# Gates of a recurrent mixer by features, convolution parameters on another queue, and a relative bias stored once

## The chip, the cores and the metric

The kernel runs on one core of a Trainium2 chip, in one launch. The metric is the device time of one execution in microseconds (us). Engines are named as the profile names them: PE is TensorE (PEld its weight loads), DVE is VectorE, ACT is ScalarE, POOL is GpSimd, and SP is SyncE, which here only issues DMAs.

## The reference, cut to what matters

Two layers over 1024 tokens of 1024 features in float32. The first layer mixes tokens by HGRN2, a gated linear recurrence with 8 heads of 128; the second by attention in a window of 128 with 16 query heads and a relative bias. Each layer ends with a gated ConvFFN (a causal convolution of width 3 in it). The parts that the change touches:

```
q, f, i, g = split(h @ w_in)                       # per head 128 columns of each
o = hgrn2_chunkwise(silu(q), 1 - fg, i, log(fg))   # i are the values V
o = o * rsqrt(mean(o**2) + eps)                    # per token and head
o = o * g_norm_w * silu(g)                         # silu(g) is the gate G
mix = o @ w_out
...
logits = q k^T * scale + bias[head, t - s]         # bias: a table of 32 buckets x 16 heads
...
u = conv(h @ w_in, conv_w) + conv_b
```

## The kernel before, in words

All activations live in SBUF (128 partitions, P = 128). Each float32 matmul of a projection is made of three products (`mm3`, lines 171 to 175: high by high, high by low, low by high) of operands that were split into a rounded high part (a cast on ACT, L154 for weights, L199 for activations) and the rest (a subtraction on DVE, L147). `T` is the input by features, high and low; `HL` is a ring of six split weight units; `raw` is a ring of three buffers for weights as they come from DRAM, loaded by SP (L142).

**The HGRN stage** takes about the first 525 us and handles the heads one after the other. For a head there are projections and a recursion. `qf` projects q and f *by features*: the weights stand in PE and 512 tokens of `T` move (`proj_T`, 24 matmuls for half of the tokens). `ig_block` projects the values V and the gate G of one head together, *by tokens*: a block of 128 tokens of `T` stands, and 256 columns of weights move, 128 of V and 128 of G (`proj_tok`, 48 matmuls for two token blocks, four such calls for a head). ACT copies V out of PSUM and makes the sigmoid of G (L694, L695), DVE multiplies it by the projection (L696). `recur`, a generator, is the recursion of a head: column sums and scores on PE (L178), levels of decay products on DVE and POOL (L854, L856, L859), masked placing (L834), states (L930, L932), and at the end the output og of eight token blocks in PSUM, squared and summed by ACT (L945), with POOL making the norm's factor ss (L946, L947), DVE multiplying by G (L948) and by ss (L949), PE transposing og (L182), and ACT scaling it by g_norm_w into Y (L956). For the last head the transposed og goes straight into the high and low parts of T (`split_scaled`, L203 on ACT and L204 on DVE). The parts of Y are then split into T (`Y_to_T`, L199 and L147) for the output projection, whose first products for other heads are made while the last head's recursion still runs.

**What sets the order.** PE's and SP's instructions run in the order in which the program writes them (`manual_schedule`); those of ACT, DVE and POOL are placed by a scheduler within their waits, except in the first block of the program, where ACT and DVE are in written order too. The recursion of head h-1 is woven between the projections of head h by the class `Order`: `od.t` is a clock that adds an estimated cost for each matmul, and after each `mm3` group `od.tick()` lets every waiting generator whose due time is reached write its next piece. A generator's `yield 8.0` is the delay to its next piece. `slot_begin` and `slot_end` put loads, stores (bsd) and sums of FFN weights between the blocks.

`conv_params` is such a generator. When the clock has come to 360, it loads the convolution's weights and biases of both layers in pieces `cr` (88 x 128, two buffers) by ACT's DMA queue, transposes each on PE (L783) and copies it (L784); then it loads rel_bias and a one-hot table, multiplies them on PE (L794) to the bias of each head by distance, and stores that to DRAM as `rbd`, 128 copies of 256 numbers for each of 16 heads (2 MB, L797). In the attention stage (about 1290 to 1455 us) SP loads for each pair of query heads a tile `bf` (L1154) whose partition p is a row shifted by p, and POOL adds it to the scores X (L1212, 32 times), before DVE takes the row maximum (L1216).

Lines of the kernel that the text names are those of the listing here.

## Time and profile before

| | |
|---|---|
| three runs | 2191.42, 2185.72, 2184.57 us |
| median | 2185.72 us |
| profiled execution | 2187.37 us, its span 2185.6 us |
| instructions | 33447 |
| PE rows in program order (matmuls, runs of equal ones merged) | 9831 |
| HGRN stage | 0 to about 525 us |

A profile page gives for each engine the time in which it had work and that time's share of the span. A line of waits reads: engine, the tile it was to write, its line, and behind the arrow what released it (engine or DMA, tile, line), then total us, number and longest. A timeline row is: start, duration, engine, line, operation, output and inputs, shape, count of equal ones in a row, and in brackets the idle time ahead of it with what ended it. A q behind an engine's name (ACTq, SPq) marks DMAs that it issues.

### The profile page before, as it was taken

Reading aid. Unit: us, or ns where it says so; the run is one execution under the profiler, and the core shown is the slowest. Engines: PE = TensorE matmul, PEld = TensorE weight load, DVE = VectorE, ACT = ScalarE, POOL = GpSimd, SP = SyncE. Lnnn points to the kernel's source line nnn. Section 1 sums busy time; section 2 is a strip of 40 time slices with the busy share of each in tenths; the row PEclk is TensorE's granted clock in tenths of the full one; section 3 lists DMA queues with packets and bytes.
Section 4 is the critical chain, followed back from the end, with each engine's and each line's share of the span. In section 5 each row is a group of like instructions: output and inputs, shape, how many; then the busy total and the mean of one; then the engine's idle time right before and its main releaser. Section 6 shows DMA issues by size and latency. Waiting matters only on the chain.

```text
span 2185.6 us, 33447 instructions
## 1 busy us (share of the span) xinstructions
PE 2149.7 (98%) x13263; PEld 1803.4 (83%) x13263; DVE 1739.9 (80%) x2291; ACT 924.5 (42%) x1573; POOL 183.2 (8%) x207
## 2 busy tenths in 40 slices
PE   8999999999999999999999999999999999999998
PEld 7888888988788888887888887778888888888887
DVE  2777666575789988988997766767899888889987
ACT  4333323342744334444343436755654444343431
POOL 0112121110100000000000022211000000000001
PEclk9999999999999999999999999999999999999999
DMA  5554443152223222227845331123123222249663
GB/s 199 192 196 174 155 174 117 59 111 95 96 69 105 87 87 87 87 81 256 298 156 168 106 100 35 35 81 122 68 97 106 78 77 78 87 154 324 202 216 130
DMA packets 231943, 281.10 MB, mean 129 GB/s; under 512 B 29977, under 2 KB 160746, under 8 KB 228970
## 3 DMA queue, kind: packets, MB, share of 16 engines
q1 hardware_dynamic: 228736, 276.53, 38.3%
q10 hardware_dynamic: 3050, 2.43, 0.9%
q8 instruction: 104, 1.70, 0.3%
q14 instruction: 53, 0.43, 0.1%
HBM read 213.90 MB, written 65.01 MB: 128 GB/s over the span
## 4 chain that ended last, share of the span: by engine, by line
PE 82%; DVE 9%; ACT 3%; DMA 3%; issue 2%; POOL 1%; SPq 0%; ACTq 0%; DVEq 0%; POOLq 0%
PE psmm L172 17%; PE psmm L173 17%; PE psmm L174 16%; PE psax L172 8%; PE psax L173 8%; PE psax L174 8%; PE psax L178 3%; PE psmm L178 1%; PE psax L1197 1%; DVE T L147 1%; PE psax L182 1%; DVE Y L477 1%; DVE HL L147 1%; DMA rx<-in_ffn_w_in_dram 1%; ACT Y L247 1%
## 5 line engine op out<-in xcount | busy, mean ns | idle before, releaser
L172 PE MATMUL psmm<-T,HL 128*128 128x512 f32 x768 | 307.5, 400 | 0.0
L173 PE MATMUL psmm<-T,HL 128*128 128x512 f32 x768 | 299.6, 390 | 4.0 <-DVE T L147 2.8
L174 PE MATMUL psmm<-T,HL 128*128 128x512 f32 x768 | 299.8, 390 | 0.0
L477 DVE SCALAR_TENSOR_TENSOR Y<-Y,cwt 128x1023 f32<-128x1023 f32 (+1 forms) x176 | 225.0, 1279 | 40.0 <-ACT Y L475 39.7
L475 ACT ACTIVATE Y<-Y,cwt 128x1024 f32<-128x1024 f32 x88 | 108.9, 1237 | 257.8 <-DVE Y L464 254.3
L172 PE MATMUL psmm<-HL,T 128*128 128x256 f32 (+1 forms) x656 | 199.8, 305 | 1.9 <-ACT T L199 1.7
L174 PE MATMUL psmm<-HL,T 128*128 128x256 f32 (+1 forms) x656 | 195.2, 297 | 1.4 <-DVE T L147 1.4
L173 PE MATMUL psmm<-HL,T 128*128 128x256 f32 (+1 forms) x656 | 195.1, 297 | 1.2 <-DVE HL L147 1.2
L199 ACT CAST HL<-rx 128x1024 fp32r<-128x1024 f32 (+1 forms) x137 | 140.2, 1046 | 124.5 <-DMA rx<-in_ffn_w_in_dram 33.6
L147 DVE TENSOR_TENSOR HL<-rx,HL 128x1024 fp32r<-128x1024 f32 (+1 forms) x137 | 165.7, 1212 | 14.5 <-ACT HL L199 14.0
L174 PEld LDWEIGHTS psmm<-T,HL 128*128 128x128 f32 x768 | 144.2, 188 | 32.4 <-issue 1.4
L173 PEld LDWEIGHTS psmm<-T,HL 128*128 128x128 f32 x768 | 144.5, 188 | 30.9 <-DVE T L147 3.5
L172 PEld LDWEIGHTS psmm<-T,HL 128*128 128x128 f32 x768 | 144.4, 188 | 30.5 <-issue 1.2
L172 PE MATMUL psax<-T,HL 128*128 128x512 f32 x352 | 137.4, 390 | 0.0
L174 PE MATMUL psax<-T,HL 128*128 128x512 f32 x352 | 137.1, 390 | 0.0
L173 PE MATMUL psax<-T,HL 128*128 128x512 f32 x352 | 137.0, 389 | 0.0
L221 POOL TENSOR_TENSOR rs<-rs,nhalf 128x1 f32<-128x1 f32 x32 | 25.9, 811 | 1305.7 <-DVE rs L220 1305.4
L172 PEld LDWEIGHTS psmm<-HL,T 128*128 128x128 f32 x656 | 126.1, 192 | 8.7 <-issue 2.5
L174 PEld LDWEIGHTS psmm<-HL,T 128*128 128x128 f32 x656 | 126.0, 192 | 5.2 <-DVE T L147 1.9
L173 PEld LDWEIGHTS psmm<-HL,T 128*128 128x128 f32 x656 | 126.2, 192 | 4.9 <-DVE HL L147 1.7
L856 POOL TENSOR_TENSOR kp<-kp,tot 128x512 f32<-128x512 f32 x48 | 73.6, 1533 | 288.3 <-PE psax L178 147.9
L147 DVE TENSOR_TENSOR HL<-raw,HL 128x1024 fp32r<-128x1024 f32 x51 | 64.2, 1258 | 21.3 <-ACT HL L154 21.3
(294 smaller groups left out, 5193.9 us busy)
## 6 DMA issues: line engine op xcount, KB each, us to landing
rx<-in_ffn_w_in_dram SPq DMA_DIRECT2D x136, 256.0 KB, 3.2
rx<-gd SPq DMA_DIRECT2D x118, 256.0 KB, 3.5
Y<-in_ffn_w_out_dram SPq DMA_DIRECT2D x44, 512.0 KB, 6.1
bsd<-Y SPq DMA_DIRECT2D x22, 1024.0 KB, 5.0
gd<-Y SPq DMA_DIRECT2D x44, 512.0 KB, 2.6
rx<-in_ffn_w_out_dram SPq DMA_DIRECT2D x54, 256.0 KB, 4.2
R<-bsd SPq DMA_DIRECT2D x44, 256.0 KB, 3.8
Y<-in_ffn_w_in_dram SPq DMA_DIRECT2D x40, 256.0 KB, 3.0
```

Source lines behind the costliest of these rows:

```text
L147: make = lambda e: e.tensor_tensor(lo, src, hi.bitcast(F32), op=ALU.subtract)
L172: nc.tensor.matmul(ps, st(0), mv(0), start=start, stop=False)
L173: nc.tensor.matmul(ps, st(0), mv(1), start=False, stop=False)
L174: nc.tensor.matmul(ps, st(1), mv(0), start=False, stop=stop)
L178: nc.tensor.matmul(ps, lhsT, rhs, start=start, stop=stop, **kw)
L182: nc.tensor.transpose(ps, src, ident)
L199: nc.scalar.copy(hi, src)
L221: nc.gpsimd.tensor_tensor(rs, rs, nhalf, op=ALU.pow)
L247: nc.scalar.activation(hf[:, kc, :], ps[:, k * P:(k + 1) * P], AF.Identity, bias=shift, scale=scale)
L475: nc.scalar.activation(c, u, AF.Identity, bias=cwt[:, l, 3, ci:ci + 1], scale=cwt[:, l, 2, ci:ci + 1])
L477: nc.vector.scalar_tensor_tensor(c[:, sh:], u[:, :S - sh], cwt[:, l, 2 - sh, ci:ci + 1], c[:, sh:], op0=ALU.mult, op1=ALU.add)
L856: (nc.gpsimd if i else nc.vector).tensor_tensor(kv[:, :, 0, :], kv[:, :, 0, :], tv[:, :, 1:2].to_broadcast([P, nb, m]), op=ALU.mult)
```

## The change

It has four parts.

1. *Gates by features.* The V of two heads is now projected together in the blocks of each even head (`v_block`, 256 columns of V of heads h and h+1), and the gates of two heads in the blocks of each odd head (`g_block`), by features: weights standing, 512 tokens moving. A head's gate is thus made by halves of the tokens, in `GT[h]` of 128 features by 1024 tokens. In the blocks of heads 1, 3 and 5 the order is both halves of head h-1, then both of head h; in those of head 7, the first halves of heads 6 and 7, then the second halves.
2. *Where the gate is applied.* og is only multiplied by ss before the transposes; the gate follows behind them. Where the gate's half is there already (odd heads), one DVE operation makes Y = transposed og * g_norm_w * G (L963 of the new kernel); where it isn't (heads 0, 2, 4, 6), ACT scales og into Y as before, and DVE multiplies Y by G after G is made (L703). For the last head the gated quarter is written over G, then cast by ACT and subtracted by DVE into T.
3. *Convolution parameters by SP.* The generator starts at 320 instead of 360; it issues all eight loads of cr (four buffers) and those of rel_bias and the one-hot table on SP's queue, and makes the transposes 12 later; rbd is stored by SP.
4. *Bias.* rbd is 16 rows of 256 numbers (16 KB), stored once, in reverse order of distance; `bias_load` reads 128 overlapping rows that start one number apart, and POOL reads bf backwards.

```diff
-            onehot[BUCKETS[(P - 1 - x) % P], x] = 1.0
+            onehot[BUCKETS[(P - 1 - x) % P], 2 * P - 2 - x] = 1.0
...
+        def v_load(h, u):
+            return load(lambda r: [(r.rearrange("p (k c) -> p k c", k=4),
+                                    w_iv[:, 4 * u:4 * u + 4, 2 * D + h * P:2 * D + (h + 2) * P])])
...
+        def v_block(h, us, tp):
+            if tp == 0:
+                VT[h] = VT[h + 1] = hp.tile([P, NB, 2, P], F32, name="V")
+            ps = psmm()
+            proj_tok(us, tp, ps)
+            return nc.scalar.copy(VT[h][:, 2 * tp:2 * tp + 2], ps.rearrange("p (t e c) -> p t e c", t=2, e=2)), None
+
+        def g_block(h, w, half):
+            if half == 0:
+                GT[h] = hp.tile([P, S], F32, name=f"G{h % 2}")
+            G = GT[h][:, half * 512:(half + 1) * 512]
+            ps = psmm()
+            proj_T(w, half, ps)
+            act = nc.scalar.activation(G, ps, AF.Sigmoid)
+            dve = nc.vector.tensor_tensor(G, G, ps, op=ALU.mult)
+            gates.add((h, half))
+            if h in turned:
+                y = Y[:, h, half * 512:(half + 1) * 512]
+                dve = nc.vector.tensor_tensor(y, y, G, op=ALU.mult)
+            return act, dve
...
         def conv_params():
-            yield 360.0
+            yield 320.0
+            crs = []
...
-                    cr = hp.tile([88, P], F32, name="cr", bufs=2)
+                    cr = hp.tile([88, P], F32, name="cr", bufs=4)
...
-                        nc.scalar.dma_start(cr[44 * j:44 * (j + 1), :], src.rearrange("(c p) -> c p", p=P))
...
+                        nc.sync.dma_start(cr[44 * j:44 * (j + 1), :], src.rearrange("(c p) -> c p", p=P))
+                    crs.append((l, k, cr))
...
+            yield 12.0
+            for l, k, cr in crs:
...
-            nc.scalar.dma_start(rbd, rl.unsqueeze(1).to_broadcast([16, P, 2 * P]))
+            nc.sync.dma_start(rbd, rl)
...
-            nc.vector.tensor_tensor(og, pv, G, op=ALU.mult)
-            between(nc.vector.tensor_tensor(og, og, ss.unsqueeze(2).to_broadcast([P, NB, P]), op=ALU.mult), 4)
+            between(nc.vector.tensor_tensor(og, pv, ss.unsqueeze(2).to_broadcast([P, NB, P]), op=ALU.mult), 4)
...
+            gated = lambda dst, ts: nc.vector.scalar_tensor_tensor(dst, ps[:, ts], par[:, 80:81], GT[h][:, ts],
+                                                                   op0=ALU.mult, op1=ALU.mult)
+            turned.add(h)
+            there = [(h, half) in gates for half in range(2)]
             if h < NH - 1:
-                nc.scalar.activation(Y[:, h, :], ps, AF.Copy, scale=par[:, 80:81])
+                for ts, gate in [(slice(0, S), there[0])] if there[0] == there[1] else [(slice(0, 512), True), (slice(512, S), False)]:
+                    if gate:
+                        gated(Y[:, h, ts], ts)
+                    else:
+                        nc.scalar.activation(Y[:, h, ts], ps[:, ts], AF.Copy, scale=par[:, 80:81])
             else:
                 for t in range(0, NB, 2):
                     ts = slice(t * P, (t + 2) * P)
-                    split_scaled(T[:, 0, h, ts], T[:, 1, h, ts], ps[:, ts], par[:, 80:81])
+                    gated(GT[h][:, ts], ts)
+                    split(T[:, 0, h, ts], T[:, 1, h, ts], GT[h][:, ts])
...
-                raws = [ig_load(h, u) for u in range(2)]
+                raws = [v_load(h, u) if h % 2 == 0 else qf_load(h - 1 + u, 3) for u in range(2)]
...
-                    slot_end(*ig_block(h, us, tp), *(make_w[tp - 1:tp] if tp else ()))
+                    u, half = (tp % 2, tp // 2) if h == NH - 1 else (tp // 2, tp % 2)
+                    done = g_block(h - 1 + u, us[u], half) if h % 2 else v_block(h, us, tp)
+                    slot_end(*done, *(make_w[tp - 1:tp] if tp else ()))
...
-            nc.sync.dma_start(bfs[c], bass.AP(tensor=rbd.tensor, offset=rbd.offset + (8 * pp + r) * 2 * P * P + P - 1,
-                                              ap=[[2 * P - 1, P], [8 * P * P, 2], [1, P]]))
+            nc.sync.dma_start(bfs[c], bass.AP(tensor=rbd.tensor, offset=rbd.offset + (8 * pp + r) * 2 * P,
+                                              ap=[[1, P], [8 * P, 2], [1, P]]))
...
-            bv = bfs[c]
+            bv = bfs[c][:, :, ::-1]
```

**What moves on the engines.** First ACT's queue at the start of the program, before (raw_94 to raw_96 are the three raw buffers, here with the first weights of V and G; psax holds the transposed blocks of x):

```order
L732 COPY warm<-nhalf 128x1
L781 DMA cr<-in_ffn_conv_w_dram 44x128
L154 CAST HL<-raw_94 128x1024
L781 DMA cr<-in_ffn_conv_w_dram 44x128 x2
L781 DMA cr<-in_ffn_conv_b_dram 44x128
L789 DMA rb<-in_rel_bias_dram 32x16
L791 DMA oh<-in_onehot_dram 32x256
L199 CAST T<-psax 128x8x128 x2
L154 CAST HL<-raw_95 128x1024
```

And ACT's queue there after the change:

```order
L740 COPY warm<-nhalf 128x1
L154 CAST HL<-raw_94 128x1024
L199 CAST T<-psax 128x8x128 x2
L154 CAST HL<-raw_95 128x1024
L154 CAST HL<-raw_96 128x1024
L199 CAST T<-psax 128x8x128 x2
L690 COPY V<-psmm 128x512
```

The six loads of convolution parameters, bias table and one-hot table have left the place ahead of the first cast of T, and so has the gate's sigmoid behind the first copy of V.

Next, SP's queue near the parameters, after the change (raw loads ahead of them are head 7's q and f weights, raw loads behind them the gate weights of heads 6 and 7; bsd is a store of summed FFN weights):

```order
L142 DMA raw_95<-in_hgrn_w_in_dram 128x8x128
L142 DMA raw_96<-in_hgrn_w_in_dram 128x8x128
L790 DMA cr<-in_ffn_conv_w_dram 44x128 x3
L790 DMA cr<-in_ffn_conv_b_dram 44x128
L790 DMA cr<-in_ffn_conv_w_dram 44x128 x3
L790 DMA cr<-in_ffn_conv_b_dram 44x128
L793 DMA rb<-in_rel_bias_dram 32x16
L795 DMA oh<-in_onehot_dram 32x256
L806 DMA rbd<-rl 16x256
L1013 DMA bsd_87<-Y 128x2048
L142 DMA raw_94<-in_hgrn_w_in_dram 128x8x128
L142 DMA raw_95<-in_hgrn_w_in_dram 128x8x128
```

Before, the same piece of SP's queue had none of them:

```order
L142 DMA raw_94<-in_hgrn_w_in_dram 128x4x128 x2
L996 DMA bsd_87<-Y 128x2048
L1001 DMA Y<-in_ffn_w_out_dram 128x1024 x2
L142 DMA raw_95<-in_hgrn_w_in_dram 128x8x128
L142 DMA raw_96<-in_hgrn_w_in_dram 128x8x128
L996 DMA bsd_87<-Y 128x2048
L142 DMA raw_94<-in_hgrn_w_in_dram 128x4x128 x2
L142 DMA raw_95<-in_hgrn_w_in_dram 128x4x128 x2
```

The seven rows with cr, rb, oh and rbd are new on SP, between a raw load and the store of bsd; the store of rbd waits for DVE's copy rl.

Last, DVE at head 7's blocks, before (Y is the mixer's output of the earlier heads, split into T; Ab holds placed scores; qp the levels' products; raw_94 and raw_96 output weights):

```order
L147 TENSOR_TENSOR T<-Y,T 128x2x512 x3
L696 TENSOR_TENSOR G<-G,psmm 128x256
L147 TENSOR_TENSOR HL<-raw_96,HL 128x1024
L147 TENSOR_TENSOR T<-Y,T 128x512
L834 COPY_PREDICATED Ab<-msk,psax 128x256
L834 COPY_PREDICATED Ab<-msk,psax 128x128
L834 COPY_PREDICATED Ab<-msk,psax 128x64x2 x2
L696 TENSOR_TENSOR G<-G,psmm 128x256
L147 TENSOR_TENSOR HL<-raw_94,HL 128x1024
L854 TENSOR_TENSOR qp<-qp,tot 128x128x4
L834 COPY_PREDICATED Ab<-msk,psax 128x256
L147 TENSOR_TENSOR HL<-raw_96,HL 128x1024
```

And after (G_4368 is head 6's gate, G_4397 head 7's):

```order
L147 TENSOR_TENSOR T<-Y,T 128x2x512 x3
L699 TENSOR_TENSOR G_4397<-G_4397,psmm 128x512
L147 TENSOR_TENSOR HL<-raw_96,HL 128x1024
L147 TENSOR_TENSOR T<-Y,T 128x512
L843 COPY_PREDICATED Ab<-msk,psax 128x256
L843 COPY_PREDICATED Ab<-msk,psax 128x128
L843 COPY_PREDICATED Ab<-msk,psax 128x64x2 x2
L147 TENSOR_TENSOR HL<-raw_96,HL 128x1024
L699 TENSOR_TENSOR G_4368<-G_4368,psmm 128x512
L703 TENSOR_TENSOR Y<-Y,G_4368 128x512
L147 TENSOR_TENSOR HL<-raw_94,HL 128x1024
L863 TENSOR_TENSOR qp<-qp,tot 128x128x4
```

The gate's products on 256 columns have become products on 512, and head 6's Y is multiplied by its gate, before the second half of Y is split into T.

More of the change, by code (lines that the diff above doesn't have):

```diff
@@ L111, in trunk @@
     gd = drp.tile([P, NF, S], F32, name="gd")
-    rbd = drp.tile([16, P, 2 * P], F32, name="rbd")
+    rbd = drp.tile([16, 2 * P], F32, name="rbd")
     bsd = [drp.tile([P, FF // 256, 2, D], F32, name=f"bsd{l}") for l in range(2)]
@@ L667, in trunk, with v_split @@
         raw_tail(raws)
-        def ig_load(h, u):
-            return load(lambda r: [(r.rearrange("p (k g c) -> p k g c", k=4, g=2)[:, :, g, :],
-                                    w_iv[:, 4 * u:4 * u + 4, (2 + g) * D + h * P:(2 + g) * D + (h + 1) * P])
-                                   for g in range(2)])
-        def ig_split(raw, eng=None):
+        def v_load(h, u):
+            return load(lambda r: [(r.rearrange("p (k c) -> p k c", k=4),
+                                    w_iv[:, 4 * u:4 * u + 4, 2 * D + h * P:2 * D + (h + 2) * P])])
+        def v_split(raw, eng=None):
             return split_raw(raw, eng).rearrange("p h (k c) -> p h k c", k=4)
@@ L733, in trunk @@
                 x_load(0)
-                raw0 = ig_load(0, 0)
+                raw0 = v_load(0, 0)
                 x_load(1)
-                raw1 = ig_load(0, 1)
+                raw1 = v_load(0, 1)
                 for tb in range(2, 4):
                     x_load(tb)
-                us = [ig_split(raw0, nc.gpsimd)]
+                us = [v_split(raw0, nc.gpsimd)]
                 x_block(0)
                 x_block(1)
-                us.append(ig_split(raw1))
+                us.append(v_split(raw1))
                 ahead = od.spawn(x_pair(2), 2.0)
-                ig_block(0, us, 0)
+                v_block(0, us, 0)
                 od.finish([ahead])
@@ L1040, in trunk @@
                 us, nw = [], {}
-                raws = [ig_load(h, u) for u in range(2)]
-                make_ig = [lambda u=u: us.append(ig_split(raws[u])) for u in range(2)]
+                raws = [v_load(h, u) if h % 2 == 0 else qf_load(h - 1 + u, 3) for u in range(2)]
+                make_ig = [lambda u=u: us.append((qf_split if h % 2 else v_split)(raws[u])) for u in range(2)]
                 steps = qf(h, w)
```

29 lines of the change are left out of this document (9 added, 20 removed).

## The prediction

> **What bounds the kernel now.** I read the busy shares first, then what TensorE waited for in the HGRN stage (the first 525 us, where nearly all of the change sits), then windows of that stage, then the rows at each place that is edited.
>
> ```profile
> PE 2149.7 (98%) x13263; PEld 1803.4 (83%) x13263; DVE 1739.9 (80%) x2291; ACT 924.5 (42%) x1573; POOL 183.2 (8%) x207
> ```
>
> TensorE (PE) is busy for 98% of the span, so an edit can pay in two ways only: less PE work, or a PE wait that goes. These are the waits of PE up to 530 us (total, number, longest):
>
> ```profile
> PE psax L182 <- DMA Y<-in_x_dram: 6.1, 2, 4.6
> PE psmm L783 <- DMA cr<-in_ffn_conv_w_dram: 2.1, 1, 2.1
> PE psmm L172 <- ACT T L199: 1.7, 1, 1.7
> PE psmm L174 <- DVE T L147: 1.4, 2, 1.0
> PE psax L178 <- DVE qp L854: 1.4, 3, 0.5
> PE psmm L173 <- issue: 1.2, 1, 1.2
> PE psmm L173 <- DVE HL L147: 1.2, 2, 0.6
> ```
>
> The first row is the arrival of x, which no edit touches. The other six hold 2.1 + 1.7 + 1.4 + 1.4 + 1.2 + 1.2 = 9.0 us: all that could come from waits here, and the change reaches about half of it. The rest has to come from PE's pace. The windows (length, then busy time and count of PE, PEld, DVE, ACT, POOL, clock, DMA share) show two stretches of one kind of matmul each, the crowded end, and the whole stage:
>
> ```profile
> 50.24:72.00 21.76, 21.76 (x97) 18.02 (x96) 12.91 (x22) 6.77 (x10) 0.00 (x0) 1.00 0.45 146
> 161.59:169.75 8.16, 8.16 (x71) 8.16 (x69) 8.03 (x11) 2.31 (x16) 1.85 (x2) 1.00 0.01 2
> 470.00:525.00 55.00, 53.49 (x551) 45.43 (x550) 29.73 (x41) 18.44 (x42) 9.68 (x7) 1.00 0.36 121
> 0.00:525.00 525.00, 508.42 (x5235) 449.98 (x5236) 324.05 (x498) 177.54 (x392) 92.62 (x75) 1.00 0.46 150
> ```
>
> DVE is busy for 324 of 525 us and ACT for 178: neither is the bound of the stage as a whole, though DVE is where waits at its end come from.
>
> **The change, part by part.**
>
> **1. Gates with 512 moving.** Each projection block is 8 slices of D by three products. For V and G of one head, before: 8 token blocks, 192 matmuls with 256 columns moving; eight heads have 1536. After, the V half stays as it is (four pairs of heads, 768 of 256 columns) and the gates are 8 heads x 2 halves x 24 = 384 matmuls of 512. So 768 short ones give way to 384 long ones; PE's rows fall by the same 384, from 9831 to 9447. The bounds of the two pure stretches are these rows:
>
> ```profile
> 50.24 0.39 PE L172 MATMUL psmm<-T,HL 128*128 128x512 f32 x1
> ...
> 72.00 0.39 PE L172 MATMUL psmm<-T,HL 128*128 128x512 f32 x1
> ...
> 161.59 0.28 PE L172 MATMUL psmm<-HL,T 128*128 128x256 f32 x1
> ...
> 169.75 0.28 PE L174 MATMUL psmm<-HL,T 128*128 128x256 f32 x1
> ```
>
> Starts are 21.76 us apart over 96 steps of the long kind, 0.2267 us a step, and 8.16 us over 68 steps of the short kind (the windows' counts, less the matmuls still running at an edge), 0.1200 us a step. A pair of short ones costs 0.2400: the long one saves 0.0133 us, and 384 of them 5.1 us. The windows say why it isn't zero: in the short stretch the weight loads (PEld) are busy for all of 8.16 us, in the long one for 18.02 of 21.76, so the short pace is that of loading weights, and half the loads go. Not every block runs undisturbed, so I take **-4.9** (bounds -3 and -5.5).
>
> The Trainium skill ("TensorE: Matmul & The Clock Gate", section "Back-to-back issue gap") speaks against this size: its formula for a warm gap is N/2.4 + 2.5 ns, by which a pair would save only 2.5 ns and the sum of this term would be about -1. The rows differ, 13.3 ns a pair, and the same section does say that its formula undercounts at small N because it has no weight load in it.
>
> **2. Convolution parameters by SyncE's queue.**
>
> ```profile
> 374.46 4.39 SPq L142 DMA_DIRECT2D raw<-in_hgrn_w_in_dram  x2
> 418.90 0.34 SPq L996 DMA_DIRECT2D bsd<-Y  x1
> ...
> 439.93 0.31 ACTq L781 DMA_DIRECT2D cr<-in_ffn_conv_w_dram  x1
> ...
> 442.95 0.27 PE L783 MATMUL psmm<-ident,cr 88*128 88x88 f32 x1 [2.11 <-DMA cr<-in_ffn_conv_w_dram]
> ```
>
> With two buffers, the second layer's loads could be issued only when the first transposes had read theirs; PE stood for 2.11 us. After, all eight loads are issued by SyncE, in four buffers, and PE comes to them 12 us of the order's clock later. SyncE runs ahead: it had issued the loads in front of this place by 379 us, and the next it issued was 40 us later. The wait goes: **-2.1** (bounds 0 and -2.1). What is queued behind: SyncE now stops at the store of rbd until DVE has copied rl, and behind that stand one store of sums and the four last raw loads of head 7, in front of which SyncE waits until 418.90 anyway for buffers; the column sums of head 6, beside which the transposes now stand, come earlier than that. If that cover were gone, head 7's gate weights would be late and PE would wait for each us of it.
>
> **3. The start.** These are rows of ACT, its DMA issues and SyncE's, and of PE in the first 25 us:
>
> ```profile
> 10.33 0.32 ACTq L791 DMA_DIRECT2D oh<-in_onehot_dram  x1
> 10.70 1.93 ACT L199 CAST T<-psax 128x1024 fp32r<-128x1024 f32 x2 [3.49 <-DMA cr<-in_ffn_conv_b_dram]
> ...
> 19.88 1.05 ACT L154 CAST HL<-raw 128x1024 fp32r<-128x1024 f32 x1 [6.31 <-DMA raw<-in_hgrn_w_in_dram]
> ...
> 8.07 1.97 PE L182 MATMUL psax<-ident,Y 128*128 128x128 f32 x8 [1.52 <-DMA Y<-in_x_dram]
> 11.76 0.58 PE L172 MATMUL psmm<-HL,T 128*128 128x256 f32 x1 [1.72 <-ACT T L199]
> ...
> 13.02 0.58 PE L174 MATMUL psmm<-HL,T 128*128 128x256 f32 x1 [0.46 <-DVE T L147]
> ...
> 23.37 0.38 PE L174 MATMUL psmm<-HL,T 128*128 128x256 f32 x1 [0.98 <-DVE T L147]
> ```
>
> ACT's queue is in order, and six of its DMA issues (cr, rb, oh) stood ahead of the first cast of T: it was free from 10.70 - 3.49 = 7.2, and cast at 10.70. After the change nothing of the kind stands there. The first block's transposes were over 1.52 before 8.07, so its cast can be over by about 8.3 and DVE's low part by 9.5; PE then goes on straight from the second block's transposes at 10.04 instead of 11.76, and at 13.02 doesn't wait: 1.72 + 0.46 = 2.18. The wait at 23.37 stands behind a raw load that landed late and a cast at 19.88; each V load is now one issue of SyncE instead of two, and ACT has no gates to do here, so most of 0.98 goes. I take **-3.0** (bounds -1, when x's arrival leaves the next wait in the place of these, and -4, when PE's slow first matmuls, 0.58 at 11.76 against 0.28 in the pure stretch, come up to pace sooner too).
>
> By Part 1 of the same page of the Trainium skill ("The HAM clock gate": full clock after about 3.4 us of sustained work) PE without a break from 8.07 would be at full pace by 12, and the sum about 1 us better; no row here shows that, and the sum doesn't hold it.
>
> **4. The end of HGRN.** Here DVE is close to full, and PE waits for it already:
>
> ```profile
> 478.68 0.75 PE L178 MATMUL psax<-qp,kp 128*32 128x32 f32 x64 [0.44 <-DVE qp L854]
> 487.47 0.50 PE L173 MATMUL psmm<-HL,T 128*128 128x512 f32 x1 [0.57 <-DVE HL L147]
> 490.76 1.09 PE L178 MATMUL psax<-qp,kp 128*32 128x64 f32 x32 [0.50 <-DVE qp L854]
> ...
> L696 DVE TENSOR_TENSOR G<-G,psmm 128x256 f32<-128x256 f32 x32 | 13.4, 418 | 35.4 <-ACT G L695 31.2 <-PE psax L178 4.0
> L818 DVE TENSOR_TENSOR qs<-qs,psmm 128x512 f32<-128x512 f32 x16 | 11.0, 686 | 24.4 <-ACT qs L817 24.3
> ```
>
> The gate's products for head 7's four blocks were 4 x 0.418 = 1.67 us of DVE; now they are 4 x 0.686 (the row of the same operation on 512 columns) and two more products of that size for head 6's halves of Y: 4.1 us, 2.4 more inside a stretch in which the recursion's levels wait for DVE. ACT has two casts of weights in a row there, of which the second waits for its load. Against that, ACT has fewer copies (no V) and Y's casts start at known points. The waits may grow from 1.5 to 4 us or shrink; elsewhere DVE's work per pair of heads is about the same, since the product with G leaves og (1.23 us a head) and comes back in the products with G. **+0.3** (bounds -1 and +4). The last head's output:
>
> ```profile
> 515.54 1.03 PE L182 MATMUL psax<-ident,og 128*128 128x128 f32 x8
> 517.12 0.48 DVE L204 SCALAR_TENSOR_TENSOR T<-psax,par,T 128x256 fp32r<-128x256 f32 x1 [4.72 <-ACT T L203]
> ```
>
> Before, each quarter is a cast by ACT and then this operation on DVE, in turn. Now DVE has eight operations, gating (of the size of this row) and subtraction (of the size of the product on 256 columns, 0.418): 4 x 0.48 + 4 x 0.42 = 3.6 us. DVE does three gatings before the first subtraction, so the first quarter is whole 3 x 0.48 + 0.42 = 1.9 us after the transposes, and PE has 15 matmuls of other work before it, 15 x 0.227 = 3.4 us. Nothing.
>
> **5. Bias.**
>
> ```profile
> 1326.35 1.30 POOL L1212 TENSOR_TENSOR X<-X,bf 128x512 f32<-128x512 f32 x1 [3.90 <-DVE X L1206]
> ...
> 1328.43 0.68 DVE L1216 TENSOR_REDUCE nm<-X 128x4 f32<-128x516 f32 x1
> 1330.51 0.50 DVE L1206 COPY_PREDICATED X<-msk,psax 128x128 f32<-128x128 uint8 x2 [1.39 <-ACT X L1201]
> ...
> L1212 POOL TENSOR_TENSOR X<-X,bf x32: 1295/1297/1305, 1291.0 to 1452.7; 128x512 f32<-128x512 f32 x32
> DMA to landing us min/median/max: 7.0/7.0/7.0
> ```
>
> The 32 additions now read bf backwards; no row shows POOL doing so. From below 1.30 us a step as now; from above double, 2.60. The next thing that needs X is DVE's maximum, 0.78 us after the addition ends here, and behind it the next masking had 1.39 idle; at double price the maximum moves by 0.5 and the masking doesn't. So **0** at either end; from about 1.30 + 0.78 + 1.39 = 3.5 on each further us costs 32. The bias loads land in 7.0 us; each serves four additions, which are (1452.7 - 1291.0)/31 = 5.2 us apart, and three buffers put it a group of four, 21 us, ahead or more; their rows overlap now but are as many and as long. The store of rbd falls from 2 MB to 16 KB, beside a stage with half its DMA time free: nothing.
>
> **The sum:** -4.9 - 2.1 - 3.0 + 0.3 = -9.7. The profiled execution took 2187.37 us (span 2185.6 and 1.8 around it); it becomes 2177.7. The median of the three runs, 2185.72, lies 1.65 below that execution, so I forecast **2176.0** for the median.
>
> **Rivals.**
> - *Part is given back* (DVE at the end of HGRN): term 4 at its dear end, +4, and the start at -1: -4.9 - 2.1 - 1 + 4 = -4.0, or 2181.7. For it: three waits on DVE in 13 us already. Against: DVE's 29.73 busy of 55.
> - *The long matmuls gain nothing much*: the short ones' 0.12 is a good stretch's and the gates' blocks are cut up by the recursion; term 1 at -1: -5.8, or 2179.9. The skill's gap formula would have it so. Against: both paces come from over 60 steps each.
> - *The wait moves*: PE no longer waits for cr but for DVE's copies of four transposes that now stand only three short matmuls apart, and for the late raw loads; term 2 becomes zero: -7.6, or 2178.1, inside the forecast's case.
> - *Slower: POOL reads backwards slowly.* It decides from 3.5 us an addition. At 4.1 us (three times as now and a bit) the 32 steps lose 0.6 each, 19 us: -9.7 + 19 = +9.5, or 2195. For it: nothing in the trace prices it. Against: POOL's 3.90 idle before the addition.
>
> **How the numbers follow.** A measurement of this kernel can tell about 0.3%, 6.6 us, from no change: faster means under 2179.2, slower above 2192.3. The forecast's case with the moved wait in it I give 0.64; part given back 0.16 and the pace alone failing 0.10, both within 0.3%; the slow addition 0.10, as the one edit whose operation no row prices. So faster 0.64, same 0.26, slower 0.10. Range: from all three gains at their best (-5.5 - 2.1 - 4 - 1 = -12.6, and 3 us for waits that shrink with them: 2170) up to the rivals within 0.3% with both prices due together (-1 - 2.1 - 1 + 4 = 0: 2186). Those two ends leave out the slower cases and little else.
>
> **What would show it.** (1) Pace: the gate's matmuls start 0.227 apart, none waits for a psmm bank held by G. (2) No wait on cr; SyncE's store of rbd before 419. (3) First T cast near 7, PE's first projection near 10.1. (4) PE's waits on qp and HL between 470 and 495 add up to under 2 us. (5) The addition's duration. I am wrong if PE waits for G or Y in the gates' blocks of odd heads, or if the start has a new wait for x or a raw load in the place of the old.

## The result, and the profile after

Six runs of the changed kernel have a median of 2177.03 us (2175.76 to 2178.92), six of the kernel before 2185.82 (2184.57 to 2191.64). The ratio of their means is 0.9953, with a 95% interval of 0.9939 to 0.9967: faster by 0.47%, which is 10.3 us by the means and 8.8 by the medians. The forecast for the median was 2176.0.

The busy shares of the changed kernel, then its PE waits up to 530 us:

```profile
PE 2142.3 (99%) x12879; PEld 1779.7 (82%) x12879; DVE 1735.6 (80%) x2281; ACT 917.1 (42%) x1535; POOL 186.2 (9%) x207
```

```profile
PE psax L182 <- DMA Y<-in_x_dram: 5.6, 2, 4.7
PE psax L178 <- DVE qp L863: 2.9, 4, 1.2
PE psmm L173 <- DVE HL L147: 0.9, 1, 0.9
PE psax L178 <- DVE og L881: 0.9, 1, 0.9
```

The waits for cr, for T at the start (twice) and the one called "issue" are gone; those for qp have doubled. The span fell by 11.1 us, from 2185.6 to 2174.5. To see where, I use instructions that both programs have: the column sums of the first and of the seventh head, and the transposes of the seventh and of the last head's og. First before, then after:

```profile
72.77 0.64 PE L178 MATMUL psax<-St,one 128*32 128x256 f32 x8
...
405.42 0.64 PE L178 MATMUL psax<-St,one 128*32 128x256 f32 x8
...
451.48 1.04 PE L182 MATMUL psax<-ident,og 128*128 128x128 f32 x8
```

```profile
68.96 0.64 PE L178 MATMUL psax<-St,one 128*32 128x256 f32 x8
...
396.10 0.64 PE L178 MATMUL psax<-St,one 128*32 128x256 f32 x8
...
439.76 1.04 PE L182 MATMUL psax<-ident,og 128*128 128x128 f32 x8
...
504.86 1.04 PE L182 MATMUL psax<-ident,og 128*128 128x128 f32 x8
```

Up to both column sums PE streams the same number of columns in both programs. The last transposes stand behind nine more long matmuls than before (9 x 0.227 = 2.04 us), which are then missing behind them.

| stretch | before | after | difference | with the nine matmuls put back |
|---|---|---|---|---|
| start to the first head's column sums | 72.77 | 68.96 | -3.81 | -3.81 |
| to the seventh head's column sums | 332.65 | 327.14 | -5.51 | -5.51 |
| to the seventh head's transposes of og | 46.06 | 43.66 | -2.40 | -2.40 |
| to the last head's (515.54 before) | 64.06 | 65.10 | +1.04 | -1.00 |
| to the end of the span | 1670.06 | 1669.64 | -0.42 | +1.62 |

So the start, the gates' pace and the parameters bring the gain, and the stages behind HGRN give 1.6 back. The waits of PE behind 530 us grow too, from 11.4 us to 13.8, by as much as in the first layer norm (0.5 before, at 570; 2.9 after, between 540 and 565).

The start after the change (ACT, then PE):

```profile
6.95 1.01 ACT L199 CAST T<-psax 128x1024 fp32r<-128x1024 f32 x1
...
9.17 0.56 PE L172 MATMUL psmm<-HL,T 128*128 128x256 f32 x1
...
11.42 0.28 PE L172 MATMUL psmm<-HL,T 128*128 128x256 f32 x1
...
13.01 0.39 PE L173 MATMUL psmm<-HL,T 128*128 128x256 f32 x1 [0.95 <-DVE HL L147]
```

T is cast at 6.95 instead of 10.70, PE projects from 9.17 instead of 11.76, and a new wait of 0.95 stands at 13.01, for the low part of the second weights, in DVE's queue behind the second block of x. PE is at its full pace from 11.42 (0.28 a matmul), before from about 15.8.

The end of HGRN (PE, then DVE):

```profile
467.13 0.75 PE L178 MATMUL psax<-qp,kp 128*32 128x32 f32 x64 [0.82 <-DVE qp L863]
471.26 0.75 PE L178 MATMUL psax<-qp,kp 128*32 128x32 f32 x64 [0.43 <-DVE qp L863]
476.54 0.70 PE L178 MATMUL psax<-qp,kp 128*32 128x32 f32 x32 [1.22 <-DVE qp L863]
```

```profile
463.58 0.68 DVE L699 TENSOR_TENSOR G<-G,psmm 128x512 f32<-128x512 f32 x1
464.29 0.96 DVE L703 TENSOR_TENSOR Y<-Y,G 128x512 f32<-128x512 f32 x1
465.18 1.21 DVE L147 TENSOR_TENSOR HL<-raw,HL 128x1024 fp32r<-128x1024 f32 x1
466.31 0.68 DVE L863 TENSOR_TENSOR qp<-qp,tot 128x512 f32<-128x512 f32 x1
```

The product qp that PE waits for at 467.13 stands on DVE behind the gate's product, the gating of Y and a weight's low part: 2.47 us of waits here, 1.51 before. POOL's addition with bf read backwards, by the rows of the tile bf:

```profile
L1231 POOL TENSOR_TENSOR X<-X,bf x32: 1290/1300/1308, 1279.2 to 1441.0; 128x512 f32<-128x512 f32 x32
```

1.300 instead of 1.297 us: reading backwards costs nothing that shows.

### The profile page after: what moved, and what is told of

Its sections match the earlier page's. It is cut to its first block, busy times and chain, and to the rows that moved or that the text cites. A ratio compares the mean times of both kernels' runs of the same rounds, so it can differ in the third digit from the quotient of the medians.

```text
span 2174.5 us, 32559 instructions
## 1 busy us (share of the span) xinstructions
PE 2142.3 (99%) x12879; PEld 1779.7 (82%) x12879; DVE 1735.6 (80%) x2281; ACT 917.1 (42%) x1535; POOL 186.2 (9%) x207
## 4 chain that ended last, share of the span: by engine, by line
PE 77%; DVE 13%; DMA 3%; ACT 3%; issue 2%; POOL 1%; SPq 0%; ACTq 0%; DVEq 0%; POOLq 0%
PE psmm L172 16%; PE psmm L174 16%; PE psmm L173 16%; PE psax L172 7%; PE psax L174 7%; PE psax L173 7%; PE psax L178 3%; DVE T L147 2%; DVE HL L147 2%; PE psmm L178 2%; PE psax L1216 1%; PE psax L182 1%; DVE Y L477 1%; ACT T L199 1%; ACT Y L247 1%
## 5 line engine op out<-in xcount | busy, mean ns | idle before, releaser
L172 PE MATMUL psmm<-T,HL 128*128 128x512 f32 x896 | 358.2, 400 | 0.0
L173 PE MATMUL psmm<-T,HL 128*128 128x512 f32 x896 | 349.2, 390 | 2.8 <-DVE T L147 2.8
L174 PE MATMUL psmm<-T,HL 128*128 128x512 f32 x896 | 349.5, 390 | 0.0
L173 PEld LDWEIGHTS psmm<-T,HL 128*128 128x128 f32 x896 | 168.6, 188 | 35.8 <-DVE T L147 3.5
L172 PEld LDWEIGHTS psmm<-T,HL 128*128 128x128 f32 x896 | 168.2, 188 | 36.1 <-issue 2.1
L174 PEld LDWEIGHTS psmm<-T,HL 128*128 128x128 f32 x896 | 168.1, 188 | 36.2
L172 PE MATMUL psmm<-HL,T 128*128 128x256 f32 (+1 forms) x400 | 126.0, 315 | 0.0
L173 PE MATMUL psmm<-HL,T 128*128 128x256 f32 (+1 forms) x400 | 122.4, 306 | 1.0 <-DVE HL L147 0.9
L174 PE MATMUL psmm<-HL,T 128*128 128x256 f32 (+1 forms) x400 | 122.2, 306 | 0.1
L199 ACT CAST HT<-rx 128x1024 fp32r<-128x1024 f32 (+1 forms) x51 | 44.0, 862 | 88.5 <-PE psmm L173 29.9
L172 PEld LDWEIGHTS psmm<-HL,T 128*128 128x128 f32 x400 | 76.9, 192 | 4.7 <-issue 1.2
L173 PEld LDWEIGHTS psmm<-HL,T 128*128 128x128 f32 x400 | 76.7, 192 | 4.8 <-DVE HL L147 1.7
```

Source lines behind the costliest of these rows:

```text
L172: nc.tensor.matmul(ps, st(0), mv(0), start=start, stop=False)
L173: nc.tensor.matmul(ps, st(0), mv(1), start=False, stop=False)
L174: nc.tensor.matmul(ps, st(1), mv(0), start=False, stop=stop)
L199: nc.scalar.copy(hi, src)
```

## The experiments

Ratios are to runs of the kernel before on the same chip, with 95% intervals; "tail" is the time from the last transposes of og to the end of the span.

**Parameters and bias alone** (the kernel before with parts 3 and 4 of the change).

> The kernel before with the last two parts of the change alone: convolution parameters by SyncE's queue (four buffers, from 320, transposes 12 later), and the bias stored once and read backwards; gates as before. By the forecast's terms: first cast of T near 7 us instead of 10.70 and PE's first projection between 9.2 and 10.1 instead of 11.76, no wait on cr, so -2.2 to -2.9 at the start and -2.1 at the parameters: 4.3 to 5.0 us faster than before (2181). Rival (the start's gain comes from V's loads in one piece and from the gates that are gone there): PE's first projection stays near 11.7, and only the 2.1 us come, 2183.7.

0.9969 (0.9958 to 0.9981), span 2180.0. PE's first projection:

```profile
9.80 0.56 PE L172 MATMUL psmm<-HL,T 128*128 128x256 f32 x1
```

The wait on cr is gone, and so is the late start, with V and G as before: the span is 5.6 us shorter (1.4 of it in the tail, which moves by as much from one profile to another). The rival falls. But the column sums come at 70.96, 1.8 us earlier than before and not 2.2 to 2.9, since the low part of the second weights keeps PE at 13.64 (0.97), and the wait at 23 us is still there (0.98 at 21.56).

**Gates alone** (parts 1 and 2; parameters on ACT's queue, bias as before).

> The kernel before with the first two parts of the change alone: gates by features and applied after the transposes; parameters by ACT's queue, bias as before. By the forecast's terms: 384 pairs at 0.0115 to 0.0133 us, -4.4 to -5.1, about +1 at the end of HGRN, the wait at 23 us gone (-1); the wait on cr and the late first cast stay: 4 to 5 us faster than before (2181). Rival (pace by the formula of the isolated gap, 2.5 ns a pair): -1 for pace and -1 for the start, 2184. Rival (the start's gain is V's): 7 to 8 us faster, with PE's first projection near 9.2.

0.9988 (0.9980 to 0.9996), span 2182.2: 3.4 us shorter, less than expected. ACT's first cast and PE's first projection:

```profile
8.71 1.93 ACT L199 CAST T<-psax 128x1024 fp32r<-128x1024 f32 x2 [1.56 <-DMA cr<-in_ffn_conv_w_dram]
```

```profile
9.77 0.58 PE L172 MATMUL psmm<-HL,T 128*128 128x256 f32 x1 [0.31 <-ACT T L199]
```

The same six DMA issues stand in front of the cast but hold it for 1.56 us instead of 3.49. A likely reason is that V's weights, which come in one load instead of two, move in fewer packets (SP's queue moved 1797 in the first 14 us, 2762 before), so that ACT's issues get through sooner; no run changes the packets alone. *Each* half of the change alone thus brings PE's start forward by 2.0 us, and both together by 2.6: the gains overlap. The 0.6 that both add is x: with nothing in the way PE projects 1.62 us after the second block's transposes begin, and these begin at 8.18 with the parameters alone, but at 7.49 here and 7.55 in the changed kernel.

The pace is all there (below), and the wait on cr stays (1.81 at 435.05). What is lost is at the end: PE waits 2.11 for a weight's low part at 480.62. ACT had begun that weight's cast at 473.27, but DVE, without a gap from 459.61, makes the low part only at 479.35, behind parts of T, a gate's product and another low part. Whether the 2-MB store on ACT's queue (from 438.55) has a share in that order is open: beside it two output weights take 14.7 us to land, but so do two in the kernel before (14.5), where PE waits 0.57. Behind the 2.11 PE's granted clock is 0.50, and the long matmuls from 482.61 to 485.60 start 0.43 us apart instead of 0.23: another 1.4 us lost.

**Four buffers for cr, nothing else** (the kernel before).

```diff
-                    cr = hp.tile([88, P], F32, name="cr", bufs=2)
+                    cr = hp.tile([88, P], F32, name="cr", bufs=4)
```

> The kernel before with four buffers for cr instead of two, nothing else: the second layer's four loads can now be issued at the start too, on ACT's queue. If ACT's queue in front of the first cast of T sets the start: the wait on cr at 443 us goes (-2.1), and PE's first projection comes 1 to 3 us later than 11.76, so 2185 to 2187, no gain. Rival (the start is set by the arrival of x and of the weights): the first projection stays near 11.8, and the kernel is 2.1 us faster.

0.9992 (0.9983 to 1.0001): no gain that the times show.

```profile
12.77 1.01 ACT L199 CAST T<-psax 128x1024 fp32r<-128x1024 f32 x1 [5.64 <-DMA cr<-in_ffn_conv_w_dram]
```

```profile
13.84 0.58 PE L172 MATMUL psmm<-HL,T 128*128 128x256 f32 x1 [3.64 <-ACT T L199]
```

The wait at 443 is gone, and PE's first projection comes 2.08 us later. Of that, 1.1 us is left at the first head's column sums (73.86 instead of 72.77), because the wait at 23 us is gone too. So the buffers alone give half of their gain back at the start; with the queue changed as well (parameters and bias alone, above) there is a gain at both places.

**Gates by features with 256 moving** (the changed kernel; each half in two passes over the weights).

```diff
-            proj_T(w, half, ps)
+            for part in range(2):
+                t0 = half * 512 + part * 256
+                for kc in range(KC):
+                    mm3(ps[:, part * 256:(part + 1) * 256], lambda i: w[:, i, kc, :], lambda i: T[:, i, kc, t0:t0 + 256],
+                        kc == 0, kc == KC - 1, n=256)
+                    od.tick()
```

> The changed kernel, with the gates by features still, but 256 tokens moving at a time: 768 short matmuls instead of 384 long ones, all else in its place. If the gain of the gates is pace, each pair costs 0.0115 to 0.0133 us more: 4.4 to 5.1 us slower than the changed kernel, 2181.5 to 2182. By the formula of the isolated gap (2.5 ns a pair): 1 us slower, 2178. If the gain comes from where the gate is applied and not from pace: no difference, 2177.

0.9967 (0.9956 to 0.9979), median 2180.47, 3.4 above the changed kernel and so somewhat less than expected. The column sums of the first and seventh head:

```profile
69.38 0.64 PE L178 MATMUL psax<-St,one 128*32 128x256 f32 x8
...
401.31 0.64 PE L178 MATMUL psax<-St,one 128*32 128x256 f32 x8
```

That stretch takes 331.93 us, 327.14 in the changed kernel. Of it 0.31 is a wait for kd and 0.69 a longer wait for og; the rest, 3.8 us over 288 pairs, is 13 ns a pair. It is pace, and not where the gate is applied. The other profiles agree: the four with gates by tokens need 331.1 to 331.3 (each less its waits for kd and for "issue"), the changed kernel's two and the gates alone 327.1 to 327.2. That is 4.0 us over 288 pairs, or 5.3 for all 384 at the same rate. Two short matmuls load weights twice and a long one once; the run doesn't part the two.

**The bias as before, on SyncE's queue** (the changed kernel with 128 copies, 2 MB, read forwards).

```diff
-            nc.sync.dma_start(rbd, rl)
+            nc.sync.dma_start(rbd, rl.unsqueeze(1).to_broadcast([16, P, 2 * P]))
```

> The changed kernel with the bias as before (128 copies of each row, 2 MB, stored by SyncE's queue, and read forwards by POOL). By the forecast: no difference, 2177, within 1 us of the changed kernel; POOL's addition stays at 1.30. Rival (the 2 MB, now in front of the store of sums and head 7's gate weights on SyncE's queue, delay them): PE waits for HL near 440 to 465 us, some 1 to 5 us slower than the changed kernel.

1.0064 (1.0051 to 1.0076), median 2202.36: 25 us slower than the changed kernel, far more than either theory had. PE's waits, and windows (length; PE, PEld, DVE, ACT, POOL busy; clock; DMA share; GB/s):

```profile
421.80 0.58 PE L173 MATMUL psmm<-HL,T 128*128 128x256 f32 x1 [10.42 <-issue]
460.25 0.50 PE L172 MATMUL psmm<-T,HL 128*128 128x512 f32 x1 [2.62 <-ACT HL L154]
467.71 0.80 PE L174 MATMUL psmm<-T,HL 128*128 128x512 f32 x1 [6.73 <-DVE HL L147]
```

```profile
407.00:412.00 5.00, 4.38 (x92) 4.00 (x92) 5.00 (x6) 0.83 (x1) 2.92 (x2) 1.00 0.83 96
412.00:417.00 5.00, 0.00 (x0) 0.00 (x0) 0.77 (x2) 1.61 (x4) 0.00 (x0) 0.69 0.83 96
417.00:422.00 5.00, 0.20 (x1) 0.20 (x2) 0.00 (x0) 0.00 (x0) 0.00 (x0) 0.50 0.84 100
422.00:427.00 5.00, 5.00 (x50) 4.71 (x51) 0.69 (x1) 0.72 (x2) 0.69 (x1) 0.50 0.91 160
```

From 411 to 422 PE does nothing, and no semaphore holds it. In the DMA view, asked in small windows, packets of the instruction queue q8 (16 KB each) pass at 397.6, 405.9 and 415.6 us in the changed kernel; here one passes at 401.4 and the next at 419.4, and 2.4 us later PE goes on. For all that time the store holds the DMA engines at a share of 0.83. That PE stood for want of code fits the counts: the profile of the kernel before has 104 such packets for 26526 matmuls and weight loads, 255 for each, and PE did 501 between the packet at 401.4 and the stall, about two packets' worth. The granted clock falls to 0.50 besides, and stays there until about 427.5. The two waits behind it are of another kind. The loads of that time are through by about 435 us, but ACT casts them only at 459.15: the scheduler, which places ACT's work when the kernel is built, put the casts behind qs and Y. The order of ACT's rows there, before and after this edit:

```
L822 ACTIVATE kp<-fg,one 128x512          L822 ACTIVATE kp<-fg,one 128x512
L826 ACTIVATE qs<-psmm 128x512            L826 ACTIVATE qs<-psmm 128x512
L154 CAST HL<-raw_94 128x1024             L954 ACTIVATE og,ss<-psax 128x128 x8
L954 ACTIVATE og,ss<-psax 128x128 x8      L819 ACTIVATE fg<-psmm 128x512
L819 ACTIVATE fg<-psmm 128x512            L820 ACTIVATE fg<-fg,lbt 128x512
L820 ACTIVATE fg<-fg,lbt 128x512          L822 ACTIVATE kp<-fg,one 128x512
L154 CAST HL<-raw_95 128x1024             L826 ACTIVATE qs<-psmm 128x512
L822 ACTIVATE kp<-fg,one 128x512          L972 ACTIVATE Y<-psax,par 128x1024
L972 ACTIVATE Y<-psax,par 128x1024        L154 CAST HL<-raw_94 128x1024
L826 ACTIVATE qs<-psmm 128x512            L154 CAST HL<-raw_95 128x1024
```

**The same store on ACT's queue**, to tell the two apart.

```diff
-            nc.sync.dma_start(rbd, rl.unsqueeze(1).to_broadcast([16, P, 2 * P]))
+            nc.scalar.dma_start(rbd, rl.unsqueeze(1).to_broadcast([16, P, 2 * P]))
```

> The changed kernel with the bias as before (2 MB), stored by ACT's queue, as before, but at the new and earlier place. Theory 1 (SyncE's queue is in order, and the gate weights stand behind the store): the waits for the gate weights' split, 6.7 and 2.6 us, go, and the 10.4 us in which PE waits for nothing that the profile shows stay or not by chance: 2177 to 2190. Theory 2 (the store fills the DMA engines whatever the queue, code for PE among what it holds up): both stay, 2197 to 2203.

1.0010 (1.0001 to 1.0019), median 2190.87:

```profile
422.19 0.58 PE L173 MATMUL psmm<-HL,T 128*128 128x256 f32 x1 [11.68 <-issue]
```

The waits for the weights are gone (the casts are in their old places), the 11.7 us without a releaser stay; here too an instruction packet passes at 398.4 and the next only at 419.9, while the store still runs; PE did 532 matmuls and weight loads in between and goes on 2.3 us after the second. Neither theory was right whole: the queue decides the weights, through the scheduler's order, and the store holds up PE on either queue, by all signs its code. And it wasn't chance: both kernels have it.

**The bias alone** (the kernel before with 16 KB stored by ACT's queue at the old place, read backwards).

> The kernel before with the last part of the change alone: 16 KB stored instead of 2 MB, by ACT's queue at the old place, and read backwards. By the prediction nothing: within 1 us of before. Rival (the 2 MB cost something where they were, too, in late output weights and PE's code): 1 to 3 us faster, with the wait of 0.57 for HL at 487 us gone.

0.9994 (0.9985 to 1.0002): nothing, and the wait at 487 us stays:

```profile
487.37 0.50 PE L173 MATMUL psmm<-HL,T 128*128 128x512 f32 x1 [0.57 <-DVE HL L147]
```

In the kernel before, the 2-MB store runs from 446 to 470 us; instruction packets pass at 446.4 and 471.6, and PE does only 381 matmuls and weight loads between them, less than two packets' worth, so it doesn't run out. The 2 MB were harmless by where they stood.

**The addition made twice.**

```diff
             nc.gpsimd.tensor_tensor(X, X, bv.unsqueeze(2).to_broadcast([P, 2, 2, P]), op=ALU.add)
+            nc.gpsimd.tensor_tensor(X, X, bv.unsqueeze(2).to_broadcast([P, 2, 2, P]), op=ALU.add)
```

> The changed kernel with POOL's addition of the bias made twice (the bias is counted twice in the output), so that POOL takes 2 x 1.30 for each of 32 steps. By the slack of the prediction (0.78 to DVE's maximum and 1.39 behind it) this costs nothing: within 1 us of the changed kernel. Rival (the 0.78 is all the slack, since the maximum holds up DVE's queue): 32 x 0.5, 17 us slower.

0.9967 (0.9955 to 0.9980), median 2180.19; the changed kernel beside it 0.9955 (0.9942 to 0.9967), 2177.60. The tail grew from 1670.9 to 1672.0. So it costs some 1 to 2.6 us, a little more than expected: nearly all is hidden, the rival's 17 are not there. DVE's waits for it in the attention stage:

```profile
DVE nm L1236 <- POOL X L1232: 8.3, 9, 2.8
```

Nine steps of 32 wait, 8.3 us in all (1.5 in the changed kernel), and little of that reaches PE.

**Head 7 in the plain order** (the changed kernel; both halves of head 6's gate, then both of head 7's).

```diff
-                    u, half = (tp % 2, tp // 2) if h == NH - 1 else (tp // 2, tp % 2)
+                    u, half = tp // 2, tp % 2
```

> The changed kernel with head 7's blocks in the order of the other odd heads: both halves of head 6's gate, then both of head 7's. If DVE's queue between 462 and 477 us is what PE waits for there, the second gating of Y moves one block ahead, out of that stretch, and a product with G of 0.68 us moves in behind: PE's waits there stay between 1.5 and 3.5 us (2.5 in the changed kernel), the time within 1 us of 2177. Rival (the halves are what feeds the output projection's first products in time): PE waits for T in the output projection's part after 477 us, 2 us or more slower.

0.9948 (0.9934 to 0.9962), median 2176.46: no difference. The waits for qp at the end are 0.22 + 0.39 + 1.19 = 1.8 instead of 2.5. "By halves" brought nothing here.

**Two waits attacked** (the changed kernel; the second V weights split between the two blocks of x, and head 6's Y gated by POOL).

```diff
                 x_block(0)
+                us.append(v_split(raw1))
                 x_block(1)
-                us.append(v_split(raw1))
...
+                if h == NH - 2:
+                    nc.gpsimd.tensor_tensor(y, y, G, op=ALU.mult)
+                else:
+                    dve = nc.vector.tensor_tensor(y, y, G, op=ALU.mult)
```

> The changed kernel with two edits: the second V weights are split between the first and the second block of x instead of after both, and head 6's Y is multiplied by its gate on POOL instead of DVE. If the waits left in the trace are what they seem: the 0.95 at 13 us (weights' low part, DVE behind x's second block) goes, and of the 2.5 us of waits for qp between 467 and 477 about 1 goes: 1 to 2 us faster than the changed kernel, 2175 to 2176. Rival (the queue fills up with the next thing): 2177, with the waits moved to x's second block and to POOL's products with kp.

0.9960 (0.9947 to 0.9973), median 2179.93: not better. The three waits for qp (2.47 together) became one for POOL's kp, which is longer:

```profile
469.87 1.08 PE L178 MATMUL psax<-qp,kp 128*32 128x32 f32 x64 [3.01 <-POOL kp L868]
```

Behind it the granted clock is 0.50 until about 473, and long matmuls start 0.43 us apart instead of 0.23. From the seventh head's transposes of og to the last head's it is 67.0 us, 65.1 and 65.2 in the changed kernel's two profiles: one long wait cost more than three short ones. At the start 0.69 us of the 0.95 stay. The rival was right.

**The changed kernel once more**, beside the next one and the doubled addition.

> The changed kernel once more, beside the others, for the spread of the start and of the stages behind HGRN: the first column sums between 69 and 70.5 us, and the time between the last transposes of og and the end within 1 us of the 1669.6 of its first profile.

Median 2177.60. First column sums at 70.27, tail 1670.87: 1.2 above the first profile, a little outside what I expected. The same program thus moves by about 1.3 us at its start and 1.2 in its tail from one profile to another.

**Last head's transposes earlier** (the changed kernel).

```diff
-            yield 8.0
+            yield 6.0 if h == NH - 1 else 8.0
```

> The changed kernel with the last head's og transposed 6 instead of 8 of the order's clock after its values, so that nine matmuls (2.0 us) stand behind the transposes instead of ahead of them. If the 1.6 us that the stages behind HGRN lose come from those nine, which no longer cover the layer norm's first parts: PE's waits between 540 and 565 (2.9 us) shrink by 1 to 2 and the kernel is 1 to 2 us faster. Rival (they come from DVE's order there, full with FFN weights): the waits stay, the time within 0.5 us.

0.9945 (0.9932 to 0.9957), median 2175.71, beside 0.9955 (0.9942 to 0.9967): 1.9 us lower, within the intervals. PE's waits in the first layer norm, in the changed kernel and here:

```profile
544.89 0.66 PE L182 MATMUL psmm<-ident,Y 128*128 128x128 f32 x4 [0.74 <-ACT Y L247]
551.27 0.66 PE L182 MATMUL psmm<-ident,Y 128*128 128x128 f32 x4 [0.25 <-ACT Y L247]
553.10 0.66 PE L182 MATMUL psmm<-ident,Y 128*128 128x128 f32 x4 [1.17 <-DVE Y L340]
560.43 0.66 PE L182 MATMUL psmm<-ident,Y 128*128 128x128 f32 x4 [0.74 <-ACT Y L247]
```

```profile
553.44 0.66 PE L182 MATMUL psmm<-ident,Y 128*128 128x128 f32 x4 [1.18 <-DVE Y L340]
560.44 0.66 PE L182 MATMUL psmm<-ident,Y 128*128 128x128 f32 x4 [0.43 <-ACT Y L247]
```

The trace shows 2.9 us of waits become 1.6, which bears out the nine matmuls as part of the cause; the kernel with 256 moving, whose transposes stand without the nine too, has 1.8. The 1.18 for DVE's Y stays in both, and no kernel with gates by tokens has it: the other part is DVE's order, the rival. The times alone don't settle a gain of this size.

## Why the prediction was right, and where it was not

- **1, pace (-4.9).** Right: 5.3, from 4.0 us over the 288 pairs between the column sums, 13.8 ns a pair where the two stretches gave 13.3. The rival of the isolated gap is out. The Trainium skill's formula ("TensorE: Matmul & The Clock Gate", section "Back-to-back issue gap") would have made the difference between 256 and 512 moving 2.5 ns a pair; the case that the same section excepts, small N with weight loads, is the one that holds.
- **2, parameters (-2.1).** Right in size: -2.40 between the seventh head's sums and its og, where no long matmul takes the place of short ones, and there is no new wait on DVE's copies; the store of rbd left SyncE at 400.51, 8.9 us before the store of sums behind it. Buffers alone take the wait away as well, but the four-buffer kernel pays for half of it at the start; the queue is what makes the gain whole.
- **3, the start (-3.0).** The first cast at 6.95 and the two waits that go are as forecast; the size is right in part by luck (-3.81 in the first profile, -2.50 in the second). The term counted on most of the 0.98 at 23 us. It is gone in the first profile, but seven of the eight profiles with this start have it still (0.65 to 0.98), the second one among them (0.97). PE also came to full pace sooner in the first profile, after nine slow matmuls instead of fourteen, worth 0.7; in the second it didn't. Against the gain stands a new wait for the second weights' low part, 0.95 and 0.39, which the sum doesn't have. What I missed besides: the gates alone, with V's weights in one load, bring PE's start forward by 2.0 us, so that the two halves' gains overlap.
- **4, the end (+0.3).** Right: PE's waits between the last two transposes of og are 2.47 instead of 2.14 (the 0.63 for HL at 456.74, ahead of the forecast's three, is gone). But the sign that I had named, under 2 us for qp and HL, didn't come: these went from 1.51 to 2.47. The stretch as a whole still gained 1.0, since 96 pairs save 1.3.
- **5, the bias (0).** Right for reading backwards (1.300 us) and for the place where the store was. Wrong in its reason: "beside a stage with half its DMA time free: nothing". At the place to which part 3 moves the store, 2 MB cost 13 us on ACT's queue and 25 on SyncE's. The small store is what lets the parameters move. I had costed the parts one by one, each against the kernel before.
- **Not in the sum.** The prediction's list of waits left out two, 0.9 for og (it stays) and 0.3 for kd (it goes), so waits held 10.2 us and not 9.0. And a wait of 1.22 us of PE without a releaser, which was in the list but in no term, goes:

```profile
304.01 0.39 PE L173 MATMUL psmm<-T,HL 128*128 128x512 f32 x1 [1.22 <-issue]
```

  All four profiles with gates by tokens have it (0.94 to 1.75), none with gates by features, not even with 256 moving, where PE has as many matmuls as before. In each of the four it ends some 2.2 to 2.4 us after an instruction packet has passed, just as the two long stalls do; here the packet passes at 301.6, while 0.6 MB moves in 2 us. So it is code on its way, by the same signs; no run changes that alone. Against it, the tail lost 1.6, which the growth of the layer norm's waits (2.4) more than covers. Its size is uncertain: in three other kernels with the old order of the last head the tail is 1667.4 to 1668.7, so that 1670.06 is the longest of four, and the loss may be 3 to 4 us.

With pace -5.3, parameters -2.4, start -3.8, code -1.2, kd -0.3, the end's waits +0.3 and the tail +1.6 the span's -11.1 is accounted for. That is one pair of profiles: by the second profile of the changed kernel the same five stretches give -2.50, -5.49, -2.37, +1.15 and +0.81, -8.4 in all. The forecast's -9.7 lies between, and misses of opposite sign (the start, the code and the tail) helped it to its 1 us.

## What to carry to other kernels

Cost the parts of a change against each other and not only against the kernel before: here two parts removed the same wait at the start, and one part was worth nothing by itself but spared another 25 us. A wait on a load may be cured by the queue that issues it, where more buffers move part of it to the place at which the issues then stand. A large store of many small pieces is judged by what else needs the DMA engines while it runs, PE's own code, it seems, among it. And three short waits of PE can be cheaper than one long one, if the clock falls behind the long one.

## What the runs showed of the hardware

- A store of 2048 pieces of 1 KB kept the DMA engines at 0.83 of their time for some 22 us at 96 GB/s; PE stood 10.4 and 11.7 us, and went on 2.4 and 2.3 us after an instruction packet of 16 KB had passed.
- After 10.4 us without work PE's granted clock was 0.50 and its short matmuls 0.21 us apart until 427.5, 5.7 us after it went on. Behind single waits of 2.11 us (gates alone) and 3.01 us (two waits attacked) it was 0.50 for some 3 us, too; behind the 2.11 us for cr in the kernel before it stayed at 1.00.
- At the start of the changed kernel full pace comes 3.9 us after the second transposes (7.55 to 11.42), about what Part 1 of the Trainium skill's page "TensorE: Matmul & The Clock Gate" has (some 3.4 us of sustained work); by that rule I had put it at 12. In the second profile it takes longer: the matmuls are still 0.21 us apart at 12.17, 4.7 us after the transposes at 7.52.
- POOL adds a tile read backwards as fast as forwards (1.300 and 1.297 us).
